# A down projection on one Trainium2 core: weights as the moving operand, and the last twelve feature tiles as six pairs with seven products each

## The chip, the cores and the metric

The kernel runs on one core of one Trainium2 chip. Its five engines have a queue each: TensorE (PE in the profile, its weight loads PEld), VectorE (DVE), ScalarE (ACT), GpSimd (POOL) and SyncE (SP, which issues most transfers). The metric is the device time of the whole program in microseconds (us); lower is better. Runs of one kernel lie within about 0.2% of each other.

## The reference

One layer of a hybrid trunk for 512 tokens of 1024 features, all in float32: token mixers, cross-attention, then a SwiGLU feed-forward block and a final RMSNorm. The change lies in the last two:

```python
gate, up = _split_cols(rmsnorm(x, norm_ffn[l]) @ w_gate_up[l], (D_FF, D_FF))   # D_FF = 2816
x = x + (jax.nn.silu(gate) * up) @ w_down[l]
return rmsnorm(x, norm_final)
```

With 128 rows to a tile, the 2816 features between the two projections are 22 tiles (`KF`), the 1024 output features are 8 (`KD`), the 512 tokens are 4 (`NT`).

## The kernel before, in words

**Precision.** Each float32 product is made of three fp32r matmuls on split operands: `hi` is the operand rounded by a ScalarE copy (L111), `lo` is what is left, a VectorE subtraction (L113), and the product is hi·hi + hi·lo + lo·hi. `split` does both. So every weight tile that arrives by DMA (`raw`) costs ScalarE one pass and VectorE one pass before TensorE can use it (`whi`, `wlo`, three buffers of 128x1024 each, as `raw`).

**Order.** TensorE's order is the order in which the program is written. `drive` runs a generator of matmul steps and, at every step, advances the pending generators once; a `side` generator is advanced at a given rate. ScalarE's, VectorE's and SyncE's instructions are placed by a scheduler at build time, and each engine then works strictly in that order.

**Gate and up projections.** Four feature tiles are computed plainly; tiles 4 to 21 are eighteen *units* (`unit`, L1211 on), each of seven Strassen products of 4 x 3 matmuls with 256 moving columns (L1221 to L1223), whose weights come in quarters. VectorE forms the sums of products from PSUM and at the end writes `gu` (L1252), one feature tile on the partitions by 512 tokens. `gu_split` splits these into `guh`, `gul`.

**Down projection, features on partitions.** For each of the eight output tiles j, `block_steps` (L128 on) runs 22 x 3 matmuls (L137 to L139): the stationary operand is a 128x128 weight tile, the moving one the 512 tokens of `guh` or `gul`. Weights come in three pieces of 8, 8 and 6 tiles. After a block, `wd_after` adds the residual (L1289) and squares the sum for the norm, and scales it by the gain (L1291). The last block is done in two halves of 256 tokens (`wd_last`), so that the end of the first half is hidden by the second.

**Final norm.** The features are on the partitions, so the sum of squares over features is itself made by matmuls with ones (L1307), then VectorE (L1311), GpSimd's power (L1313), a matmul that spreads the row over the partitions (L1317), four VectorE multiplications (L1321) and four output transfers (L1322), for each half.

**Buffers.** `G("a")`, `G("b")`, `G("c")` are pools of 16, 16 and 8 tiles of 128x512, `V` one of 20; `TMP` takes small rotating pools, of which "c" has three tiles. PSUM has eight banks: `PM` 3, `PS` 2, `PD` 3.

Of the kernel before, what the change touches and what calls it, by code (L numbers as in the profile page):

```python
# [40 lines left out]
def hybrid_block(  # L41
    ctx: ExitStack,
    tc: tile.TileContext,
    xT, xN, memT, memN, consts, wz0, wz, wq, wk, wv, wqb, wkb, wvb, wga, wgb,
    w_a, w_b, bias, w_o, w_mq, w_mk, w_mv, w_mo, w_g, w_u, w_d, outT,
):
    nc = tc.nc
    ctx.enter_context(tc.manual_schedule(engines={mybir.EngineType.PE}))
# [26 lines left out]
    def TMP(name, tag, bufs=None, shape=(P, T), dt=F32, pool=None):  # L75
        return (pool or tp).tile(list(shape), dt, tag="t" + tag, bufs=bufs or TB[tag], name=nm(name))
# [12 lines left out]
    def PS(name):  # L89
        return PSUM("ms", name)  # L90
# [16 lines left out]
    def gain(c, k):  # L107
        return cst[:, c + k : c + k + 1]
# [19 lines left out]
    def block_steps(ps, src, act, kt=KD, pieces=None, n=slice(0, T), eng=None):  # L128

        pieces = pieces or [(0, kt)]  # L130
        w = n.stop - n.start
        for a, b in pieces:
            hi, lo = weights(src[:, a:b, :] if (a, b) != (0, kt) else src, b - a, P, eng)
            for k in range(a, b):
                xh, xl = act[k]
                first, last = k == 0, k == kt - 1
                nc.tensor.matmul(out=ps[:, :w], lhsT=hi[:, k - a, :], rhs=xh[:, n], start=first, stop=False)  # L137
                nc.tensor.matmul(out=ps[:, :w], lhsT=hi[:, k - a, :], rhs=xl[:, n], start=False, stop=False)  # L138
                nc.tensor.matmul(out=ps[:, :w], lhsT=lo[:, k - a, :], rhs=xh[:, n], start=False, stop=last)  # L139
                yield  # L140
# [1142 lines left out]
    x4 = x3
    acc4 = TMP("acc", "acc")
    PIECES = [(0, 8), (8, 16), (16, KF)]
    dps = {}

    def wd_after(j):
        nc.vector.tensor_tensor(out=x4[j], in0=dps[j], in1=x4[j], op=ALU.add)  # L1289
        square_sum(acc4, x4[j], j)  # L1290
        nc.scalar.activation(x4[j], x4[j], AF.Copy, scale=gain(C_FIN, j))  # L1291
        yield

    def wd_last(j, tok, ps, sq):
        yield from block_steps(ps, w_d[j], gu, kt=KF, pieces=PIECES, n=tok)
        nc.vector.tensor_tensor(out=x4[j][:, tok], in0=ps[:, :H], in1=x4[j][:, tok], op=ALU.add)
        q = TMP("sq", "th")
        nc.scalar.activation(q[:, :H], x4[j][:, tok], AF.Square)
        sq.append(q)
        nc.scalar.activation(x4[j][:, tok], x4[j][:, tok], AF.Copy, scale=gain(C_FIN, j))  # L1300

    def final(tok, sq):
        yield from wait(6)
        ps = [PS("r4") for _ in range(2)]
        for i, q in enumerate([acc4[:, tok]] + sq):
            for tt in range(2):
                nc.tensor.matmul(out=ps[tt][:, 0:1], lhsT=q[:, tt * P : tt * P + P], rhs=ones[:, 0:1],  # L1307
                                 start=(i == 0), stop=(i == len(sq)))
        var, rs = SM("r4", 2), SM("r4", 2)
        for tt in range(2):  # L1310
            nc.vector.tensor_scalar(out=var[:, tt : tt + 1], in0=ps[tt][:, 0:1], scalar1=1.0 / D, scalar2=EPS,  # L1311
                                    op0=ALU.mult, op1=ALU.add)
        nc.gpsimd.tensor_tensor(out=rs, in0=var, in1=mhalf[:, :2], op=ALU.pow)  # L1313
        yield from wait(4)
        pr = PS("row4")
        for tt in range(2):
            nc.tensor.matmul(out=pr[:, tt * P : tt * P + P], lhsT=rs[:, tt : tt + 1].to_broadcast([P, P]), rhs=ident,  # L1317
                             start=True, stop=True)
        for i in (3, 0, 1, 2):
            x = x2t[i][:, :, tok]  # L1320
            nc.vector.tensor_tensor(out=x, in0=x, in1=pr[:, :H].unsqueeze(1).to_broadcast([P, 2, H]), op=ALU.mult)  # L1321
            (nc.scalar if i in (0, 2) else nc.sync).dma_start(out=outT[i][:, :, tok], in_=x)  # L1322

    wd = series(w_d, dps, gu, wd_after, range(KD - 1), kt=KF, pieces=PIECES)
    side = gu_splits(range(13, KF))
    drive(wd[0], side=side)
    drive(*wd[1:])
    for hf in range(2):
        tok, sq = slice(hf * H, hf * H + H), []
        drive(*[(wd_last(j, tok, PM("wd"), sq), None) for j in (KD - 1,)])  # L1330
        pending.append(final(tok, sq))
# [73 lines left out]
```

## Time and profile before

| | us |
|---|---|
| median of three runs | 1207.29 (1205.94 to 1208.83) |
| the profiled execution | 1206.24 |
| its span, from the first to the last instruction | 1204.5 |
| eighteen units, each | 10.1 |
| first matmul of the down projection | at 1071.56 |
| seven whole blocks | 1071.5 to 1176.7 |
| the last block, in two halves | 1176.7 to 1194.0 |
| end of the last matmul of the projection to the end of the span | 10.5 |

Times inside the execution count from the first instruction. The profile names an instruction by source line, engine, operation and tiles (out<-in). A busy TensorE is not a TensorE at its peak: matmuls overlap, so that the duration of one (390 ns) is longer than the distance between two starts, and it is the distance that adds up.

### The profile page before, as it was taken

To read this page: it belongs to the slowest core of one execution; us is meant where nothing else is said; L and a number is where in the kernel's file an instruction comes from. 1 tells how busy PE (TensorE), PEld (TensorE's weight loads), DVE (VectorE), ACT (ScalarE), POOL (GpSimd) and SP (SyncE) were. 2 spreads that over 40 slices of the span, in tenths; PEclk is the share of its full clock that TensorE was granted. 3 is DMA by queue.
4 is the path that set the end of the run, shared out by engine and by line. 5 is a ranking of instruction groups with operands and counts; after the bars stand their busy time and mean duration, and the time that the engine had idled before them with its cause. 6 is when DMAs were issued, how large, how long until landed. Compare 5 with 4: busy or idle time off the path is not lost.

```text
span 1204.5 us, 19433 instructions
## 1 busy us (share of the span) xinstructions
PE 1190.0 (99%) x7461; PEld 1040.0 (86%) x7461; DVE 757.4 (63%) x1550; ACT 579.8 (48%) x1195; POOL 140.4 (12%) x140
## 2 busy tenths in 40 slices
PE   9999999999999999999999999999999999999997
PEld 8788888899998887777788898888889999998886
DVE  5977783356543487875465564446888998892223
ACT  7573334355742376765333453335544555462222
POOL 0031331120110000000022200002021111100000
PEclk9999999999999999999999999999999999999998
DMA  8253335111343432223324453113267777633333
GB/s 284 88 167 119 127 109 138 62 54 58 125 142 125 164 114 81 88 89 113 112 98 125 130 175 122 54 36 123 79 169 195 188 179 189 160 107 103 97 96 101
DMA packets 72044, 147.04 MB, mean 122 GB/s; under 512 B 18928, under 2 KB 27536, under 8 KB 71952
## 3 DMA queue, kind: packets, MB, share of 16 engines
q1 hardware_dynamic: 65680, 135.32, 35.9%
q0 software_dynamic: 5184, 9.44, 4.6%
q8 instruction: 58, 0.95, 0.3%
q10 hardware_dynamic: 1088, 1.05, 0.3%
q14 instruction: 34, 0.28, 0.1%
HBM read 137.90 MB, written 7.88 MB: 121 GB/s over the span
## 4 chain that ended last, share of the span: by engine, by line
PE 92%; DVE 3%; DMA 2%; ACT 1%; issue 1%; POOL 0%; POOLq 0%; SPq 0%; DVEq 0%; ACTq 0%
PE g L137 6%; PE g L139 6%; PE g L138 6%; PE fp L1223 5%; PE fp L1222 5%; PE fp L1221 5%; PE nat L162 3%; PE nat L164 2%; PE nat L163 2%; PE pt L821 2%; PE ob L829 2%; PE qa L137 1%; DMA raw<-in_wz 1%; PE kb L137 1%; PE ff L137 1%; PE gb L137 1%
## 5 line engine op out<-in xcount | busy, mean ns | idle before, releaser
L111 ACT ACTIVATE whi<-raw 128x1024 fp32r<-128x1024 f32 (+4 forms) x220 | 203.1, 931 | 309.6 <-PE g L138 91.3
L113 DVE TENSOR_TENSOR wlo<-raw,whi 128x1024 fp32r<-128x1024 f32 (+4 forms) x206 | 225.1, 1098 | 152.2 <-ACT whi L111 151.6
L1223 PE MATMUL fp<-fh,wlo 128*128 128x256 f32 x504 | 142.7, 283 | 0.1
L1221 PE MATMUL fp<-fh,whi 128*128 128x256 f32 x504 | 142.6, 283 | 0.0
L1222 PE MATMUL fp<-fl,whi 128*128 128x256 f32 x504 | 142.6, 283 | 0.0
L1223 PEld LDWEIGHTS fp<-fh,wlo 128*128 128x128 f32 x504 | 96.7, 192 | 0.3 <-DVE wlo L113 0.3
L1221 PEld LDWEIGHTS fp<-fh,whi 128*128 128x128 f32 x504 | 96.8, 192 | 0.0
L1222 PEld LDWEIGHTS fp<-fl,whi 128*128 128x128 f32 x504 | 96.8, 192 | 0.0
L111 ACT ACTIVATE whi<-fs 128x512 fp32r<-128x512 f32 x72 | 42.4, 624 | 54.0 <-PE fp L1222 28.4
L203 POOL TENSOR_TENSOR acc<-acc,sq 128x512 f32<-128x512 f32 x18 | 28.8, 1600 | 299.0 <-ACT sq L202 167.8
L138 PE MATMUL g<-gul,whi 128*128 128x512 f32 x154 | 60.1, 390 | 0.0
L139 PE MATMUL g<-guh,wlo 128*128 128x512 f32 x154 | 60.1, 390 | 0.0
L137 PE MATMUL g<-guh,whi 128*128 128x512 f32 x154 | 60.1, 390 | 0.0
L162 PE MATMUL nat<-whi,hh 128*128 128x256 f32 x192 | 57.1, 298 | 0.4 <-DVE conv L391 0.4
L164 PE MATMUL nat<-wlo,hh 128*128 128x256 f32 x192 | 54.3, 283 | 0.0
L163 PE MATMUL nat<-whi,hl 128*128 128x256 f32 x192 | 54.2, 282 | 0.0
L113 DVE TENSOR_TENSOR wlo<-fs,whi 128x512 fp32r<-128x512 f32 x72 | 48.0, 686 | 5.5 <-ACT whi L111 4.7
L799 ACT ACTIVATE P<-P,mx 128x128 f32<-128x128 f32 (+1 forms) x64 | 35.9, 561 | 30.0 <-DVE mx L797 29.8
L113 POOL TENSOR_TENSOR wlo<-raw,whi 128x1024 fp32r<-128x1024 f32 x14 | 34.0, 2428 | 105.3 <-ACT whi L111 105.3
L162 PEld LDWEIGHTS nat<-whi,hh 128*128 128x128 f32 x192 | 36.7, 191 | 0.9 <-issue 0.6
L163 PEld LDWEIGHTS nat<-whi,hl 128*128 128x128 f32 x192 | 36.7, 191 | 0.0
L164 PEld LDWEIGHTS nat<-wlo,hh 128*128 128x128 f32 x192 | 36.6, 191 | 0.0
(419 smaller groups left out, 3275.4 us busy)
## 6 DMA issues: line engine op xcount, KB each, us to landing
raw<-in_w_g SPq DMA_DIRECT2D x22, 512.0 KB, 4.4
fs<-in_w_u SPq DMA_DIRECT2D x36, 256.0 KB, 2.9
raw<-in_w_d SPq DMA_DIRECT2D x18, 512.0 KB, 3.5
raw<-in_w_u SPq DMA_DIRECT2D x18, 256.0 KB, 5.0
fs<-in_w_u POOLq DMA_DIRECT2D x18, 256.0 KB, 5.8
fs<-in_w_g POOLq DMA_DIRECT2D x18, 256.0 KB, 5.6
raw<-in_wk SPq DMA_DIRECT2D x8, 512.0 KB, 4.0
raw<-in_wga SPq DMA_DIRECT2D x8, 512.0 KB, 3.7
```

The lines of the kernel that those rows point to most:

```text
L111: nc.scalar.activation(hi, src, AF.Copy, scale=1.0 if scale is None else scale)
L113: (eng or nc.vector).tensor_tensor(out=lo, in0=src, in1=hi.bitcast(F32), op=ALU.subtract)
L137: nc.tensor.matmul(out=ps[:, :w], lhsT=hi[:, k - a, :], rhs=xh[:, n], start=first, stop=False)
L138: nc.tensor.matmul(out=ps[:, :w], lhsT=hi[:, k - a, :], rhs=xl[:, n], start=False, stop=False)
L139: nc.tensor.matmul(out=ps[:, :w], lhsT=lo[:, k - a, :], rhs=xh[:, n], start=False, stop=last)
L162: nc.tensor.matmul(out=o, lhsT=xh[:, tok], rhs=hi[:, kw, :], start=(k == 0), stop=False)
L163: nc.tensor.matmul(out=o, lhsT=xl[:, tok], rhs=hi[:, kw, :], start=False, stop=False)
L164: nc.tensor.matmul(out=o, lhsT=xh[:, tok], rhs=lo[:, kw, :], start=False, stop=(k == KD - 1))
L799: nc.scalar.activation(pr, pr, AF.Exp, scale=-1.0, bias=mx, accum_out=rs[:, t : t + 1])
L1221: nc.tensor.matmul(out=o, lhsT=hi[:, k, :], rhs=xh, start=k == 0, stop=False)
L1222: nc.tensor.matmul(out=o, lhsT=hi[:, k, :], rhs=xl, start=False, stop=False)
L1223: nc.tensor.matmul(out=o, lhsT=lo[:, k, :], rhs=xh, start=False, stop=k == 3)
```

## The change

The stationary operand is now the activation, 128 features by 128 tokens, and the moving operand 512 output features of the weights (`w_d` is laid out as 22 tiles of 128x1024). The output has tokens on the partitions: eight banks hold four token tiles times two feature halves, called quads a, b, c, d of two banks each, and all stay open through the whole projection.

- `plain_down`: feature tiles 0 to 9, each times eight banks, three matmuls each (`triple`).
- Tiles 10 to 21 are six pairs. A pair is a 2x2 block product: 256 tokens by 128 features by 512 outputs a piece, done with seven products (of two token tiles, three matmuls each) where eight stood. `down_first` has four products for each pair, `down_second` the other three; `middle` moves sums between quads from PSUM with VectorE.
- Activation sums are prepared by `preps` beside `plain_down`; weight sums (`t3`, the second half of `raw`, `t2s`) by VectorE inside `down_first`.
- `take_part` empties the eight banks of the plain sum into `part` tiles together with the residual, so that the residual must have tokens on partitions too: `natural_x3` transposes it by 32 TensorE transposes, four in each of eight units, and ScalarE copies them back.
- The final norm works per partition: ScalarE squares and sums along the row (`accum_out`), VectorE adds, GpSimd takes the power, and one scale per row half follows. It runs for each token tile by itself (`final`); the output is stored as 512x1024.

Where instructions went. VectorE in a plain block of the down projection, before; `x` is the residual tile, `g` the PSUM bank of the block:

```order
L1289 TENSOR_TENSOR x_0_6700<-g_11587,x_0_6700 128x512
L113 TENSOR_TENSOR wlo_11775<-raw_11772,whi_11774 128x768
L113 TENSOR_TENSOR wlo_11800<-raw_11797,whi_11799 128x1024
L113 TENSOR_TENSOR wlo_11835<-raw_11832,whi_11834 128x1024
L1289 TENSOR_TENSOR x_0_6700<-g_11708,x_0_6700 128x512
```

and in `down_first` of the change, from the third pair's first sum on; `w_2427` and `w_2436` are the lower right weight tiles (`w22`) of the third and fourth pair, `w_2416`, `w_2425` and `w_2434` the lower left ones (`w21`) of the first, second and third, `t_` is `t3`:

```order
L1389 TENSOR_TENSOR t_2428_12186<-raw_12184,w_2427_12185 128x512
L1409 TENSOR_TENSOR t2s_12089<-t2s_12089,w_2416_12123 128x512
L1409 TENSOR_TENSOR t2s_12145<-t2s_12145,w_2425_12169 128x512
L1390 TENSOR_TENSOR raw_12184<-raw_12184 128x512
L1394 TENSOR_TENSOR t2s_12191<-raw_12184,w_2427_12185 128x512
L113 TENSOR_TENSOR wlo_12193<-raw_12184,whi_12192 128x1024
L1389 TENSOR_TENSOR t_2437_12232<-raw_12230,w_2436_12231 128x512
L113 TENSOR_TENSOR wlo_12198<-t_2428_12186,whi_12197 128x512
L113 TENSOR_TENSOR wlo_12198<-t2s_12191,whi_12197 128x512
L1390 TENSOR_TENSOR raw_12230<-raw_12230 128x512
L1409 TENSOR_TENSOR t2s_12191<-t2s_12191,w_2434_12215 128x512
```

Where a block of 66 matmuls had four VectorE rows, a pair of 24 matmuls has seven: one of 1024 columns and six of 512. `w_2436` lies in the buffer that `w_2425` held, so its transfer can start only after the third row.

TensorE in a unit, in the second product of the unit, before:

```order
L1221 MATMUL fp_9575<-fh_8605,whi_9516 128x256
L1222 MATMUL fp_9575<-fl_8606,whi_9516 128x256
L1223 MATMUL fp_9575<-fh_8605,wlo_9517 128x256
L1221 MATMUL fp_9575<-fh_8607,whi_9516 128x256
L1222 MATMUL fp_9575<-fl_8608,whi_9516 128x256
L1223 MATMUL fp_9575<-fh_8607,wlo_9517 128x256
```

and in the change; `x3n` is the PSUM bank that takes the transposed residual tile `x_1`:

```order
L1221 MATMUL fp_9587<-fh_8605,whi_9528 128x256
L1222 MATMUL fp_9587<-fl_8606,whi_9528 128x256
L1223 MATMUL fp_9587<-fh_8605,wlo_9529 128x256
L1301 MATMUL x3n_9599<-ident,x_1_6701 128x128 x4
L1221 MATMUL fp_9587<-fh_8607,whi_9528 128x256
L1222 MATMUL fp_9587<-fl_8608,whi_9528 128x256
L1223 MATMUL fp_9587<-fh_8607,wlo_9529 128x256
```

Four transposes stand between two matmul triples of one product; eight units have them.

The diff, cut to its core:

```diff
-            tag = "c" if j < 5 or j == KF - 1 else "a" if j < 13 else "b"
+            tag = "c" if j < 5 else "a"
...
+    NPL, NSP = 10, 6
+    HOME = ("bbbbbbb", "bbbbbbb", "vvvvvvv", "vvvvvvv", "aaaaaab", "vvvvccb")
+    def preps(js):
+        for i in js:
+            top, bot = gf[NPL + 2 * i], gf[NPL + 2 * i + 1]
+            x11, x21, x12, x22 = top[:, lh], top[:, rh], bot[:, lh], bot[:, rh]
...
+            tt(out=u[:, lh], in0=x21, in1=x22, op=ALU.subtract)
+            tt(out=u[:, rh], in0=u[:, lh], in1=x11, op=ALU.subtract)
+            split(tiles[0], tiles[1], u)
+            tt(out=v[:, lh], in0=x11, in1=x21, op=ALU.subtract)
+            tt(out=v[:, rh], in0=u[:, rh], in1=x12, op=ALU.add)
+            split(tiles[6][:, lh], tiles[6][:, rh], x11)
+            split(tiles[2], tiles[3], v)
+            split(tiles[4], tiles[5], bot)
...
+    def natural_x3(j):
+        pt = PS("x3n")
+        for t in range(NT):
+            nc.tensor.transpose(out=pt[:, t * P : t * P + P], in_=x3[j][:, t * P : t * P + P], identity=ident)
+        yield
+        nc.scalar.activation(x3[j], pt, AF.Copy)
...
+        if 5 <= j < 5 + KD:
+            pending.append(seq(wait(6), natural_x3(j - 5)))
...
+    def triple(o, act, w, t, **kw):
+        for i, (x, y) in enumerate(((0, 0), (1, 0), (0, 1))):
+            nc.tensor.matmul(out=o, lhsT=act[x][:, tok], rhs=w[y], start=start and i == 0, stop=stop and i == 2, **kw)
...
+    def plain_down():
+        for k in range(NPL):
+            raw, hi, lo = (pair_tile(t) for t in ("raw", "whi", "wlo"))
+            nc.sync.dma_start(out=raw, in_=w_d[k].rearrange("p (x f) -> p x f", x=2))
+            split(hi, lo, raw)
+            for n, q in enumerate("ccbbaadd" if k else "acdacdbb"):
...
+                triple(banks[q][t], gu[k], (hi[:, hf, :], lo[:, hf, :]), tok0 + t, start=k == 0, stop=k == NPL - 1)
+                if k == NPL - 1 and n % 2:
+                    pending.append(take_part(q))
...
+    def down_first():
+        for i in range(NSP):
+            ra, w22, t3 = pair_tile("raw"), TMP("w22", "c"), TMP("t3", "th")
...
+            tt(out=t3, in0=a[1], in1=w22, op=ALU.add)
+            tt(out=a[1], in0=a[0], in1=a[1], op=ALU.add)
+            split(ha, la, ra)
+            tt(out=t2s[i], in0=a[1], in1=w22, op=ALU.add)
+            split(hb[:, 1, :], lb[:, 1, :], t3)
+            split(hb[:, 0, :], lb[:, 0, :], t2s[i])
+            for q, act, hi, lo, x in (("c", op["x11"], ha, la, 0), ("b", op["s1"], ha, la, 1),
+                                      ("a", op["s3"], hb, lb, 1), ("d", op["s2"], hb, lb, 0)):
+                for t in range(2):
+                    triple(banks[q][t], act, (hi[:, x, :], lo[:, x, :]), t, start=i == 0, stop=i == NSP - 1)
...
+                if q == "b":
+                    nc.sync.dma_start(out=w21, in_=bot[:, :T])
+                    tt(out=t2s[i], in0=t2s[i], in1=w21, op=ALU.add)
...
+    def middle():
+        for t in range(2):
+            tt(out=keep[2 + t], in0=p["b"][t], in1=keep[2 + t], op=ALU.subtract)
+        for t in range(2):
+            tt(out=keep[t], in0=p["d"][t], in1=keep[t], op=ALU.add)
+        for t in range(2):
+            for n, o, op in (("a", t, ALU.add), ("d", t, ALU.subtract), ("d", 2 + t, ALU.add), ("b", t, ALU.subtract)):
+                tt(out=r[n][t], in0=r[n][t], in1=keep[o], op=op)
...
+    def last_sum(n, x):
+        if q != "d":
+            tt(out=r, in0=r, in1=banks[q][n % 2], op=ALU.add)
+        nc.scalar.activation(junk, r, AF.Square, scale=1.0 / 32, accum_out=ssq[n][:, x : x + 1])
+        tt(out=r, in0=r, in1=grow[x], op=ALU.mult)
...
+    def final(n):
+        nc.vector.scalar_tensor_tensor(out=v, in0=ssq[n][:, 0:1], scalar=EPS, in1=ssq[n][:, 1:2],
+                                       op0=ALU.add, op1=ALU.add)
+        nc.gpsimd.tensor_tensor(out=rs, in0=v, in1=mhalf[:, :1], op=ALU.pow)
+        nc.scalar.activation(r[1], r[1], AF.Copy, scale=rs)
+        nc.scalar.dma_start(out=outN[n * P : n * P + P, T:], in_=r[1])
+        nc.vector.tensor_scalar(out=r[0], in0=r[0], scalar1=rs, scalar2=None, op0=ALU.mult)
+        nc.sync.dma_start(out=outN[n * P : n * P + P, :T], in_=r[0])
...
+    drive((plain_down(), None), side=seq(gu_splits(range(6, NPL)), preps(range(NSP))), rate=0.55, delay=2)
+    drive((down_first(), middle()))
+    drive((down_second(), final(1)))
```

`down_second` takes, in this order: the fourth weight product (`t2s`) of pairs 0 and 1 into quad a; the lower weights of pair 0 into quads b and c; the fourth of pair 2; the lower weights of pair 1; and so on, with the last three pairs' lower weights token tile by token tile at the end. Removed are `wd_after`, `wd_last` and the old `final` with everything said of them above.

More of the change, by code (lines that the diff above doesn't have):

```diff
@@ L1277, in hybrid_block @@
             pending.append(seq(wait(8), gu_splits([j - 9])))
+        if 5 <= j < 5 + KD:
+            pending.append(seq(wait(6), natural_x3(j - 5)))
         if j == KF - 2:
-            pending.append(seq(wait(10), gu_splits(range(5, 9)), wait(8), gu_splits(range(9, 13))))
+            pending.append(seq(wait(10), gu_splits([5])))
     flush()
[L1283 to L1291, printed above, removed]
-        yield
@@ L1294, in wd_last @@
[L1294 to L1331, printed above, removed]
+    banks = {"a": [PM("wda"), PM("wda")], "c": [PD("wdc"), PD("wdc")], "d": [PS("wdd"), PS("wdd")],
+             "b": [PM("wdb"), PD("wdb")]}
+    quad = {"c": (0, 0), "b": (0, 1), "a": (2, 0), "d": (2, 1)}
@@ new lines, in hybrid_block, with halves, pair_tile @@
+    part = {n: [G("c", "part") for _ in range(2)] for n in "cb"}
+    keep = [TMP("keep", "ti") for _ in range(4)]
+    grow = [TMP("grow", t) for t in ("rrow", "acc")]
+    def halves(t):
+        return [t[:, x, :] for x in range(2)]
+    def pair_tile(tag):
+        return wp.tile([P, 2, T], F32 if tag == "raw" else F32R, tag=tag, bufs=3, name=nm(tag))
+    def triple(o, act, w, t, **kw):
+        tok = slice(t * P, t * P + P)
+        start, stop = kw.pop("start"), kw.pop("stop")
+        for i, (x, y) in enumerate(((0, 0), (1, 0), (0, 1))):
+            nc.tensor.matmul(out=o, lhsT=act[x][:, tok], rhs=w[y], start=start and i == 0, stop=stop and i == 2, **kw)
@@ new lines, in old, with view, take_part @@
+    def old(q, t, x):
+        tok0, hf = quad[q]
+        o = (tok0 + t) * P
+        return x2t[2 * hf + x][:, :, o : o + P]
+    def view(t, x):
+        return t[:, x * H : x * H + H].rearrange("p (e f) -> p e f", e=2)
+    def take_part(q):
+        if q in "ad":
+            part[q] = [G("a", "part") for _ in range(2)]
+        for t in range(2):
+            r, ps = part[q][t], banks[q][t]
+            if q in "cb":
+                for x in range(2):
+                    tt(out=view(r, x), in0=view(ps, x), in1=old(q, t, x), op=ALU.add)
+            else:
+                nc.scalar.activation(r, ps, AF.Copy)
+        yield
+        if q in "ad":
+            for t in range(2):
+                for x in range(2):
+                    tt(out=view(part[q][t], x), in0=view(part[q][t], x), in1=old(q, t, x), op=ALU.add)
+                yield
@@ new lines, in hybrid_block @@
+    t2s = {}
+    def down_first():
+        for x in range(2):
+            nc.sync.dma_start(out=grow[x], in_=gfin[:, x * T : x * T + T])
+        for i in range(NSP):
+            top, bot = w_d[NPL + 2 * i], w_d[NPL + 2 * i + 1]
+            ra, w22, t3 = pair_tile("raw"), TMP("w22", "c"), TMP("t3", "th")
+            nc.sync.dma_start(out=ra, in_=top.rearrange("p (x f) -> p x f", x=2))
+            nc.sync.dma_start(out=w22, in_=bot[:, T:])
+            a = halves(ra)
+            tt(out=t3, in0=a[1], in1=w22, op=ALU.add)
+            tt(out=a[1], in0=a[0], in1=a[1], op=ALU.add)
+            t2s[i] = G("a", "t2s")
+            ha, la = pair_tile("whi"), pair_tile("wlo")
+            split(ha, la, ra)
+            tt(out=t2s[i], in0=a[1], in1=w22, op=ALU.add)
+            hb, lb = pair_tile("whi"), pair_tile("wlo")
+            split(hb[:, 1, :], lb[:, 1, :], t3)
+            split(hb[:, 0, :], lb[:, 0, :], t2s[i])
+            op = ops_[i]
+            for q, act, hi, lo, x in (("c", op["x11"], ha, la, 0), ("b", op["s1"], ha, la, 1),
+                                      ("a", op["s3"], hb, lb, 1), ("d", op["s2"], hb, lb, 0)):
+                for t in range(2):
+                    triple(banks[q][t], act, (hi[:, x, :], lo[:, x, :]), t, start=i == 0, stop=i == NSP - 1)
+                    if i == NSP - 1 and q in "ca":
+                        nc.scalar.activation(keep[t + 2 * (q == "a")], banks[q][t], AF.Copy)
+                    yield
+                if q == "b":
+                    w21 = TMP("w21", "c")
+                    nc.sync.dma_start(out=w21, in_=bot[:, :T])
+                    tt(out=t2s[i], in0=t2s[i], in1=w21, op=ALU.add)
@@ new lines, in middle @@
+    def middle():
+        p, r = banks, part
+        for t in range(2):
+            tt(out=keep[2 + t], in0=p["b"][t], in1=keep[2 + t], op=ALU.subtract)
+        yield from wait(12)
+        for t in range(2):
+            tt(out=keep[t], in0=p["d"][t], in1=keep[t], op=ALU.add)
+            yield
+        for t in range(2):
+            for n, o, op in (("a", t, ALU.add), ("d", t, ALU.subtract), ("d", 2 + t, ALU.add), ("b", t, ALU.subtract)):
+                tt(out=r[n][t], in0=r[n][t], in1=keep[o], op=op)
+                yield
@@ new lines, in down_second, with fourth, load, one @@
+    def down_second():
+        ws, w4 = {}, []
+        def fourth(i):
+            if i % 2 == 0:
+                w4[:] = pair_tile("whi"), pair_tile("wlo")
+            w = tuple(z[:, i % 2, :] for z in w4)
+            split(w[0], w[1], t2s[i])
+            for t in range(2):
+                triple(banks["a"][t], ops_[i]["x22"], w, t, start=False, stop=i == NSP - 1, skip_group_check=True)
+                yield
+        def load(i):
+            raw, hi, lo = (pair_tile(t) for t in ("raw", "whi", "wlo"))
+            nc.sync.dma_start(out=raw, in_=w_d[NPL + 2 * i + 1].rearrange("p (x f) -> p x f", x=2))
+            split(hi, lo, raw)
+            ws[i] = hi, lo
+        def one(i, t, x):
+            hi, lo = ws[i]
+            q, o = (("c", "x12"), ("b", "s4"))[x]
+            triple(banks[q][t], ops_[i][o], (hi[:, x, :], lo[:, x, :]), t, start=False, stop=i == NSP - 1,
+                   skip_group_check=True)
+            yield
+        def both(i, t):
+            yield from one(i, t, 1)
+            yield from one(i, t, 0)
+        yield from fourth(0)
+        yield from fourth(1)
+        for i in range(NSP - 3):
+            load(i)
+            for t in range(2):
+                yield from both(i, t)
+            if i + 2 < NSP:
+                yield from fourth(i + 2)
+        for i in range(NSP - 1, NSP):
+            yield from fourth(i)
+        pending.append(seq(final(2), final(3)))
+        for i in range(NSP - 3, NSP):
+            load(i)
+            yield from both(i, 0)
+        pending.append(final(0))
+        for x in (1, 0):
+            for i in range(NSP - 3, NSP):
+                yield from one(i, 1, x)
@@ new lines, in hybrid_block @@
+    ssq = {}
+    def last_sum(n, x):
+        lh_ = n < 2
+        q = ("c", "b")[x] if lh_ else ("a", "d")[x]
+        r = part[q][n % 2]
+        if q != "d":
+            tt(out=r, in0=r, in1=banks[q][n % 2], op=ALU.add)
+        if n not in ssq:
+            ssq[n] = SM("ssq", 2, tag="ssq", bufs=4)
+        junk = TMP("sqj", "th")
+        nc.scalar.activation(junk, r, AF.Square, scale=1.0 / 32, accum_out=ssq[n][:, x : x + 1])
+        tt(out=r, in0=r, in1=grow[x], op=ALU.mult)
+        return r
@@ new lines, in final @@
+    def final(n):
+        r = {}
+        for x in (1, 0):
+            r[x] = last_sum(n, x)
+        yield
+        v, rs = SM("r4", 1, tag="r4v", bufs=4), SM("r4", 1, tag="r4s", bufs=4)
+        nc.vector.scalar_tensor_tensor(out=v, in0=ssq[n][:, 0:1], scalar=EPS, in1=ssq[n][:, 1:2],
[5 more added lines that the diff above has]
+        nc.sync.dma_start(out=outN[n * P : n * P + P, :T], in_=r[0])
+        yield
@@ L1403 @@
     got = r.results[0]["out_0"]
[L1404 removed]
+    return _np.ascontiguousarray(got).reshape(1, T, D)
```

26 lines of the change are left out of this document (21 added, 5 removed).

## The prediction

> **What bounds the kernel now.** First the page: each engine's share of the span, and the span in 40 slices of 30.1 us.
>
> ```profile
> PE 1190.0 (99%) x7461; PEld 1040.0 (86%) x7461; DVE 757.4 (63%) x1550; ACT 579.8 (48%) x1195; POOL 140.4 (12%) x140
> ...
> PE   9999999999999999999999999999999999999997
> DVE  5977783356543487875465564446888998892223
> PEclk9999999999999999999999999999999999999998
> ```
>
> TensorE is full until the last slice, at full clock; VectorE is at 8 to 9 tenths in the units and at 2 to 3 in the down projection. Then the waits of TensorE over the last 440 us, longest first:
>
> ```profile
> PE row L1317 <- POOL r L1313: 1.0, 1, 1.0
> PE r L1307 <- ACT sq L1298: 0.7, 1, 0.7
> ```
>
> Only the final norm keeps it waiting, so before that the time is the number of matmuls times their distance. For the distance, the busy time by windows: whole blocks, the last block, the tail (columns: us, then busy us and instructions of PE, PEld, DVE, ACT, POOL, then clock, DMA share, GB/s).
>
> ```profile
> 1071.50:1176.70 105.20, 105.20 (x464) 86.80 (x464) 37.09 (x44) 33.76 (x43) 6.48 (x5) 1.00 0.33 98
> 1176.70:1194.00 17.30, 17.30 (x147) 17.26 (x147) 8.21 (x12) 5.99 (x8) 2.00 (x2) 1.00 0.25 82
> 1194.00:1204.50 10.50, 2.07 (x13) 1.60 (x11) 3.22 (x7) 0.92 (x2) 0.70 (x1) 0.64 0.41 142
> ```
>
> Seven blocks are 462 matmuls of 512 columns in 105.2 us: one every 0.2277 us. The last block, 132 of 256 columns and some of the norm's, takes 17.3. The projection takes 122.5 us, the tail 10.5.
>
> **Part by part: TensorE.** Afterwards 10 tiles x 8 banks x 3 = 240 matmuls and 6 pairs x 7 products x 2 x 3 = 252, all of 512 columns with a new stationary tile each, as now. 492 x 0.2277 = 112.0 us, 10.5 less: 36 matmuls fewer are 8.2, and 66 long ones for the last block (15.0 for 17.3) are 2.3.
>
> **The 32 transposes** are new in the full units. The same form stands in the attention part (start, us, what):
>
> ```profile
> 504.25 0.60 PE L821 MATMUL pt<-ident,P 128*128 128x128 f32 x4
> 504.61 0.37 PE L794 MATMUL sc<-kA,qA 128*128 128x256 f32 x1
> ...
> 508.06 0.38 PE L821 MATMUL pt<-ident,P 128*128 128x128 f32 x2
> 508.19 0.48 PE L794 MATMUL sc<-kA,qA 128*128 128x512 f32 x1
> ```
>
> Four hold TensorE for 0.36 us, two for 0.13, so 32 cost between 2.1 and 2.9; I take 2.9, from the group of the same size. One lasts longer than that:
>
> ```profile
> L821 PE MATMUL pt<-ident,P x160: 270/272/330, 441.0 to 577.9; 128*128 128x128 f32 x160
> ```
>
> but they overlap. The Trainium skill ("TensorE: Matmul & The Clock Gate", Part 4: PE-mode transpose) gives about 275 ns for a transpose in one kernel's context; taken as the price of each it would be 8.8 us, 5.9 more. By that rule the trace agrees on the duration and not on the price of a group. ScalarE's copy of each result (0.62 us) waits in order for the transposes, and the weight splits behind it wait too. What hides that is ScalarE's idle time in a unit, in brackets:
>
> ```profile
> 968.01 1.15 ACT L111 ACTIVATE whi<-fs 128x512 fp32r<-128x512 f32 x2 [1.42 <-issue]
> 970.89 1.15 ACT L111 ACTIVATE whi<-fs 128x512 fp32r<-128x512 f32 x2 [1.73 <-issue]
> ```
>
> 1.4 to 1.7 us twice and more in 10: nothing. With that cover gone, 0.6 us x 8 units would be 5.
>
> **VectorE in the pairs.** Here the cover is thin. The prices, by kind (busy us, mean ns):
>
> ```profile
> L113 DVE TENSOR_TENSOR wlo<-raw,whi 128x1024 fp32r<-128x1024 f32 x18 | 22.0, 1224 | 58.8 <-ACT whi L111 58.8
> L113 DVE TENSOR_TENSOR wlo<-fs,whi 128x512 fp32r<-128x512 f32 x32 | 21.4, 686 | 2.4 <-ACT whi L111 1.9 <-PE fp L1222 0.4
> L111 ACT ACTIVATE whi<-raw 128x1024 fp32r<-128x1024 f32 x18 | 19.1, 1061 | 52.3 <-PE g L138 45.2 <-issue 3.3 <-PE wd L138 2.4
> L111 ACT ACTIVATE whi<-fs 128x512 fp32r<-128x512 f32 x32 | 18.8, 624 | 24.3 <-PE fp L1222 14.4 <-issue 9.9
> L1289 DVE TENSOR_TENSOR x<-g,x 128x512 f32<-128x512 f32 x7 | 4.8, 691 | 13.9 <-PE g L139 13.9
> ```
>
> and how close they follow each other where VectorE is full:
>
> ```profile
> 1004.78 0.68 DVE L1191 TENSOR_TENSOR fs<-fs,raw 128x512 f32<-128x512 f32 x1
> 1005.50 0.69 DVE L1192 TENSOR_TENSOR fs<-raw,fs 128x512 f32<-128x512 f32 x1
> 1006.11 1.28 DVE L113 TENSOR_TENSOR wlo<-raw,whi 128x512 fp32r<-128x512 f32 x2
> ...
> 1010.40 0.41 DVE L1247 TENSOR_TENSOR fU<-fU,fp 128x256 f32<-128x256 f32 x1
> 1010.73 0.41 DVE L1248 TENSOR_TENSOR fcc<-fW,fp 128x256 f32<-128x256 f32 x1
> ```
>
> L1192 reads what L1191 wrote and starts 0.72 us after it; the next row, which needs neither, starts 0.61 later; 256 columns take 0.33. So I count 0.60 for 512 columns, 0.33 for 256, 0.72 where a row reads the one ahead, and 1.13 for 1024 (1.22 less the same 0.09). The Trainium skill ("VectorE: DVE Perf Modes", The DRAIN you can't avoid) has it that the next operation doesn't start until the pipeline is empty; by that rule every row costs its whole duration, and the time is that of the first rival below. The trace agrees for the dependent row only.
>
> A pair: 1.13 + 6 x 0.60 + 0.12 = 4.85 us of VectorE in 24 x 0.2277 = 5.46 of TensorE. It keeps up, with 0.6 a pair. Three places are tight.
>
> (1) Entering: VectorE can't run ahead, for the first pair's second split goes into the buffer of plain tile 8 (from 0), released 24 matmuls or 5.46 us before the plain part ends; with 0.2 for the matmul's own end and ScalarE's pass of 0.62, VectorE starts 4.6 ahead of that end. Up to the first pair's last `lo` stand 14 rows of 256 (the plain sums with the residual), 5 of 512 and one of 1024: 4.62 + 3.0 + 1.13 = 8.75 us, to 4.15 after the end. TensorE wants it after 20 matmuls, 4.55. It fits by 0.4.
>
> (2) `w22` of pairs four to six waits for a buffer that `t2s += w21` frees, three rows ahead of the sum `t3` that needs it (0.60, 0.72 for the one that reads it, 1.13, and about 0.5 of waiting for ScalarE's pass of 1.06 between, an estimate): 2.9 us. The transfers:
>
> ```profile
> raw<-in_w_d SPq DMA_DIRECT2D x18, 512.0 KB, 3.5
> ...
> fs<-in_w_u SPq DMA_DIRECT2D x36, 256.0 KB, 2.9
> raw<-in_w_u SPq DMA_DIRECT2D x18, 256.0 KB, 5.0
> ```
>
> 256 KB land in 2.9 where the queue is quiet, in 5.0 in the busy units. The pairs are quiet: just in time.
>
> (3) In `down_second` the first lower weights go into a buffer that is free when pair six is half done, 2.7 us before its end; 0.2 and ScalarE's pass of 1.06 later, 1.45 before the end, VectorE goes on. Then stand 1.13 + 4 x 0.62 (PSUM, `middle`) + 8 x 0.60 + 1.13 = 9.5 us ahead of the second lower weights' `lo`, that is 8.1 after the pair's end, where TensorE wants it after 32 matmuls, 7.3. It waits 0.8.
>
> I take 1.0 us of waiting in all: bounds are 0 and the 3.8 that full durations give. `preps` and the splits beside it (6 rows of 1024, 18 of 512, 28 of 256: 26.8 us of VectorE in the 54.6 of 240 matmuls) hide.
>
> **The tail.** Now it is this chain:
>
> ```profile
> 1194.08 0.42 DVE L1296 TENSOR_TENSOR x<-wd,x 128x256 f32<-128x256 f32 x1 [1.41 <-PE wd L139]
> 1194.60 0.42 ACT L1298 ACTIVATE sq<-x 128x256 f32<-128x256 f32 x1 [8.16 <-DVE x L1296]
> 1195.95 0.70 POOL L1313 TENSOR_TENSOR r<-r,mhalf 128x2 f32<-128x2 f32 x1 [6.86 <-DVE r L1311]
> 1197.88 2.48 DVE L1321 TENSOR_TENSOR x<-x,row 128x512 f32<-128x512 f32 x4 [2.01 <-PE row L1317]
> ```
>
> From the end of L1321 (1200.36) to the span's end are 4.1 us of output. The two small matmul steps and three of four multiplications go. Afterwards: about 1.0 for VectorE's queue (it serves token tiles 2, 3 and 0 in the last 10 us), the sum 0.69, ScalarE's square 0.62, the add (under 0.2), the power 0.70, the scale 0.62 and 4.1 for the output are 7.9, and 6 handovers of some 0.15 make 8.9; I take 9.0, 1.5 less.
>
> **Sum.** -10.5 + 1.0 + 2.9 - 1.5 = -8.1 on the profiled execution's 1206.24 (span 1204.5): 1198.1. The median of the runs lies 1.05 above that execution: 1199.2.
>
> **The rivals.**
> - *VectorE pays whole durations.* A pair is then 1.22 + 6 x 0.69 = 5.36 of 5.46; entering takes 14 x 0.41 + 5 x 0.69 + 1.22 = 10.4 and is late by 1.3; place (3) takes 10.7 and waits 2.0; with no slack left the late transfers of place (2) show, 0.5. That is 3.8, 2.8 over the forecast, and the tail's queue adds 0.7: 1202.7. For it: many rows of a pair read the one ahead. Against: rows that don't start 0.60 to 0.61 apart.
> - *Slower: the `w22` transfers lead.* VectorE then stands 3 x (landing - 2.9 - 0.6), TensorE behind it. At 5.0 us that is 4.5, 1203; it decides the sign from 6.2 on; at 7.5 it is 12: 1210. For it: SyncE issues in order, and three half loads stand between whole ones. Against: 3.5 us for 512 KB in this very stage.
> - *Transposes cost their duration*: 32 x 0.272 = 8.7, 5.8 more: 1205.0, no change. Against it: the 0.36 us.
> - *Everything fits*: no waiting, tail without queue (8.0), transposes 2.1: 2.8 less, 1196.4.
>
> **Chances.** Forecast 0.50, whole durations 0.20, everything fits 0.14, transposes 0.05, `w22` 0.06, and 0.05 for some cost in the units that eats the gain. Measurements of this kernel tell about 0.2% (2.4 us) from no change. Faster are the first three, 0.84; slower `w22`, 0.06; the rest 0.10. The range takes the first three, with the runs' own spread of 1.4 about the outer ones: 1195.0 to 1204.2.
>
> **What would show it.** The plain part at 54.6 us; TensorE waiting for VectorE's `wlo` near the second lower weights and little elsewhere; units longer by 0.36 in eight of eighteen; the last output issued some 5.5 us after the last matmul. Wrong if TensorE waits over 4 us in the pairs, for `wlo` behind `t3` (then `w22`) or behind back-to-back rows (then durations), or if the units grow by over 0.5 each.

## The result, and the profile after

The change runs in 1198.06 us (median of four runs, 1197.57 to 1198.93), the kernel before in 1206.80 (four runs, 1205.94 to 1208.83): a ratio of 0.9926, with a 95% interval of 0.9909 to 0.9943. The forecast was 1199.2. The profiled execution took 1197.57 us and has a span of 1195.9.

The page: engines' shares, and the span in 40 slices of 29.9 us, to be held against the same rows of before.

```profile
PE 1180.9 (99%) x7367; PEld 1029.3 (86%) x7367; DVE 805.2 (67%) x1652; ACT 598.0 (50%) x1238; POOL 135.1 (11%) x136
...
PE   9999999999999999999999999999999999999997
DVE  5977783356543388875365564546788898899687
PEclk9999999999999999999999999999999999999999
```

TensorE is as full as before. VectorE's last four slices, 2 to 3 tenths before, are now 6 to 9. Then the busy time by windows, cut at the first matmul of the units, at the first one of the projection, at the pairs, at `down_second` and at the end of the last matmul:

```profile
888.89:1074.10 185.21, 185.11 (x1546) 184.90 (x1544) 164.03 (x312) 99.73 (x196) 28.11 (x32) 1.00 0.70 177
1074.10:1128.97 54.87, 54.87 (x242) 45.06 (x241) 40.46 (x77) 23.89 (x38) 0.00 (x0) 1.00 0.30 97
1128.97:1162.06 33.09, 33.09 (x145) 27.04 (x144) 29.85 (x47) 15.95 (x26) 0.00 (x0) 1.00 0.54 167
1162.06:1187.75 25.69, 25.27 (x109) 20.00 (x107) 23.04 (x38) 13.55 (x25) 1.51 (x2) 1.00 0.30 103
1187.75:1195.90 8.15, 0.00 (x0) 0.00 (x0) 2.78 (x6) 2.06 (x4) 1.47 (x2) 0.67 0.34 129
```

and of before the row that answers to the first:

```profile
889.78:1071.56 181.78, 181.68 (x1513) 181.47 (x1512) 163.24 (x312) 97.18 (x192) 27.95 (x32) 1.00 0.70 176
```

The stages side by side, in us:

| | forecast | before | after | difference |
|---|---|---|---|---|
| units, with the transposes | +2.9 | 181.78 | 185.21 | +3.43 |
| projection, first start to last end | -9.5 | 122.48 | 113.65 | -8.83 |
| tail | -1.5 | 10.46 | 8.15 | -2.31 |
| sum | -8.1 | 314.72 | 307.01 | -7.71 |

The two executions also differ by 0.89 us ahead of the units (888.89 against 889.78), where no instruction of the change stands. A start that is compared between executions carries that: the projection's first matmul is only 2.54 us later, and the units are 3.43 longer. So the stages are compared by their lengths, not by when they begin.

TensorE's waits in units, projection and tail, and those of its weight loads in the projection:

```profile
PE wdb L1338 <- DVE wlo L113: 0.4, 1, 0.4
PEld wdb L1338 <- DVE wlo L113: 0.8, 1, 0.8
```

One wait, at the place (3) of the prediction: the matmuls stand idle 0.4 us there, the weight loads 0.8.

### The profile page after: what moved, and what is told of

It reads as the page before. It is cut to its first block, busy times and chain, and to the rows that moved or that the text cites. A ratio compares the mean times of both kernels' runs of the same rounds, so it can differ in the third digit from the quotient of the medians.

```text
span 1195.9 us, 19401 instructions
## 1 busy us (share of the span) xinstructions
PE 1180.9 (99%) x7367; PEld 1029.3 (86%) x7367; DVE 805.2 (67%) x1652; ACT 598.0 (50%) x1238; POOL 135.1 (11%) x136
## 4 chain that ended last, share of the span: by engine, by line
PE 90%; issue 4%; DVE 3%; DMA 2%; ACT 1%; SPq 0%; POOL 0%; POOLq 0%; DVEq 0%
PE fp L1223 5%; PE fp L1221 5%; PE fp L1222 5%; PE g L137 3%; PE g L139 3%; PE g L138 3%; PE nat L162 3%; PE wdb L1338 3%; PE nat L163 2%; PE nat L164 2%; PE wda L1338 2%; PE wdc L1338 2%; PE wdd L1338 2%; PE pt L821 2%; PE ob L829 2%
## 5 line engine op out<-in xcount | busy, mean ns | idle before, releaser
L111 ACT ACTIVATE whi<-raw 128x1024 fp32r<-128x1024 f32 (+3 forms) x215 | 199.7, 937 | 272.3 <-issue 65.2
L113 DVE TENSOR_TENSOR wlo<-raw,whi 128x1024 fp32r<-128x1024 f32 (+3 forms) x201 | 221.6, 1107 | 99.6 <-ACT whi L111 98.7
L799 ACT ACTIVATE P<-P,mx 128x128 f32<-128x128 f32 (+1 forms) x64 | 35.9, 561 | 30.1 <-DVE mx L797 29.9
L203 POOL TENSOR_TENSOR acc<-acc,sq 128x512 f32<-128x512 f32 x12 | 21.6, 1800 | 172.7 <-issue 131.0
L797 DVE CUSTOM_DVE_ANT_0 P<-sc,bias 128x128 f32<-128x128 f32 (+1 forms) x64 | 31.0, 484 | 4.8 <-PE sc L795 4.2
L1189 POOL DMA_DIRECT2D fs<-in_w_g x18 | 15.8, 875 | 120.8 <-DVE fs L1191 33.6
L137 PE MATMUL qa<-hh,whi 128*128 128x512 f32 x64 | 28.7, 448 | 0.0
```

Of the source, the lines that this page charges most:

```text
L111: nc.scalar.activation(hi, src, AF.Copy, scale=1.0 if scale is None else scale)
L113: (eng or nc.vector).tensor_tensor(out=lo, in0=src, in1=hi.bitcast(F32), op=ALU.subtract)
L799: nc.scalar.activation(pr, pr, AF.Exp, scale=-1.0, bias=mx, accum_out=rs[:, t : t + 1])
```

## The experiments

### Without the transposes

```diff
-        if 5 <= j < 5 + KD:
-            pending.append(seq(wait(6), natural_x3(j - 5)))
```

> The change without the 32 transposes of the residual and without ScalarE's eight copies of them, so that the residual that is added has features where tokens belong. The theory, by the 0.32 us that a group of four added between the units' matmuls: the first matmul of the projection comes 2.5 us earlier than with the change (about 1071.6 instead of 1074.1), the time is about 1195.5. The rival, by the 272 ns that one transpose lasts: 8.7 us earlier, about 1189.4.

Measured: 1195.01 us, ratio to the kernel before 0.9898 (0.9879 to 0.9916), 3 to 4 us under the change. Its units:

```profile
888.25:1070.05 181.80, 181.70 (x1513) 181.49 (x1512) 163.35 (x312) 95.48 (x188) 27.93 (x32) 1.00 0.71 179
```

181.80 is the length before to 0.02, so the transposes, with ScalarE's copies, cost 185.21 - 181.80 = 3.41 us, 0.427 a group and 0.107 each. The projection's first matmul comes 4.05 us earlier, but 0.64 of that lies ahead of the units. The rival's 8.7 falls; but the theory's 2.5, and the bounds of 2.1 to 2.9 in the prediction, were too low. Why shows in the change's rows round a group (start, us, what):

```profile
932.82 0.28 PE L1223 MATMUL fp<-fh,wlo 128*128 128x256 f32 x1
932.94 0.60 PE L1301 MATMUL x3n<-ident,x 128*128 128x128 f32 x4
933.29 0.37 PE L1221 MATMUL fp<-fh,whi 128*128 128x256 f32 x1
933.50 0.28 PE L1222 MATMUL fp<-fl,whi 128*128 128x256 f32 x1
933.62 0.28 PE L1223 MATMUL fp<-fh,wlo 128*128 128x256 f32 x1
```

From the first transpose to the next matmul's start are 0.35 us, which is what the prediction read in the attention part (0.36). But that matmul holds TensorE for 0.21 where its neighbours hold it for 0.12: part of the group's cost comes out behind it. The attention part of the kernel before shows the same in the row behind the two that the prediction read:

```profile
504.81 0.28 PE L795 MATMUL sc<-klz,qA 128*128 128x256 f32 x1
```

The matmul at 504.61 holds TensorE for 0.20, also at 256 columns. With the 0.08 over 0.12 the group costs 0.44, and eight of them 3.5, close to the 3.41. The distance must be taken to the second start behind a group.

### All plain, tokens on the partitions

`plain_all` takes the place of `plain_down`, `down_first`, `middle` and `down_second`; its first 19 feature tiles run like this, the last three token tile by token tile.

```diff
-    drive((down_first(), middle()))
-    drive((down_second(), final(1)))
+        for k in range(KF - 3):
+            for n, q in enumerate("ccbbaadd" if k else "acdacdbb"):
+                triple(banks[q][t], gu[k], (hi[:, hf, :], lo[:, hf, :]), tok0 + t, start=k == 0, stop=False)
...
+    drive((plain_all(), final(1)), side=gu_splits(range(6, KF)), rate=0.55, delay=2)
```

> All 22 feature tiles plain, with tokens on the partitions, the weights moving, the transposes and the new norm as in the change; no pairs, no sums of weights or activations, no sums between banks. The theory (36 more matmuls at 0.228 us, and no wait or longer distance in the pairs to set against them): the projection takes 528 x 0.2277 = 120.2 us where the change takes 113.65, the tail as with the change or 0.3 longer: about 1204.8, 2 us under the kernel before. The rival that the seven products are eaten by what VectorE and ScalarE do for them: within 1.5 us of the change, about 1198 to 1199.5.

Measured: 1207.50 us, ratio 0.9998 (0.9984 to 1.0013): no different from the kernel before, and 9 us over the change. In its profiled execution the stages ahead of the units, which are the same, took 5.9 us longer than in the change's (its granted clock was 0.83 from 80 to 100 us, 1.00 in the change's), so it is read from the units on: units, projection, tail.

```profile
894.74:1079.94 185.20, 185.09 (x1545) 184.89 (x1544) 164.05 (x312) 101.37 (x200) 27.93 (x32) 1.00 0.69 175
1079.94:1200.26 120.32, 120.32 (x530) 99.00 (x528) 41.66 (x58) 30.76 (x42) 1.50 (x2) 1.00 0.26 86
1200.26:1209.60 9.34, 0.00 (x1) 0.00 (x0) 4.43 (x12) 3.55 (x8) 1.64 (x2) 0.65 0.37 140
```

The projection is as expected: 528 matmuls, 120.32 us. The tail is 1.2 longer than the change's (its last sums are two VectorE rows of 256 columns each instead of one of 512, and one of them waits for a tile that an output still reads). The total missed the expected 1204.8 by 2.7 us: the longer tail is 0.9 to 1.2 of that, the rest lies in the ten runs' spread (1204.59 to 1211.37), which is wider than the change's. From the units on it takes 314.86 us, the kernel before 314.72. So the turned operands alone bring nothing: 2.2 us off the projection (the last block in 512 columns) and 1.1 off the tail are paid back by 3.4 for the transposes. The gain is that of the seven products: 113.65 for 120.32, -6.67 of the 8.2 that 36 matmuls are worth. The rival that they are eaten falls.

### Two more VectorE rows in each pair

```diff
             tt(out=t2s[i], in0=a[1], in1=w22, op=ALU.add)
+            for _ in range(2):
+                tt(out=xtra, in0=t2s[i], in1=grow[0], op=ALU.add)
```

> The change with two more VectorE sums of 128x512 in each pair of the first products; nobody reads their result. It asks how much of a pair VectorE has left. The theory (rows start 0.60 us apart): a pair is 4.85 + 1.20 = 6.05 us of VectorE in 5.46 to 5.58 of TensorE, so TensorE waits 0.5 to 0.6 a pair, less what slack there is at the start, 2.0 to 4.0 us in all: about 1200 to 1202. The rival (rows cost their whole duration): 5.36 + 1.38 = 6.74, 1.2 us a pair, 7 us or more: about 1205 or later. Waits of TensorE would name VectorE's lo of the pair weights in both.

Measured: 1201.29 us, ratio 0.9953 (0.9939 to 0.9967), 3.2 over the change; the projection takes 117.37 us, 3.72 more. TensorE's waits and those of its weight loads:

```profile
PE wdc L1339 <- DVE wlo L113: 1.6, 4, 0.7
PE wdb L1339 <- DVE wlo L113: 1.0, 1, 1.0
```

```profile
PEld wdc L1339 <- DVE wlo L113: 3.3, 4, 1.1
PEld wdb L1339 <- DVE wlo L113: 1.4, 1, 1.4
PEld wdd L1339 <- DVE wlo L113: 0.5, 1, 0.5
```

and one pair of VectorE, from one second extra row (L1397) to the next:

```profile
1143.71 0.69 DVE L1397 TENSOR_TENSOR xtra<-t2s,grow 128x512 f32<-128x512 f32 x1
1144.32 0.69 DVE L113 TENSOR_TENSOR wlo<-t,whi 128x512 fp32r<-128x512 f32 x1
1144.92 0.69 DVE L113 TENSOR_TENSOR wlo<-t2s,whi 128x512 fp32r<-128x512 f32 x1
1145.52 0.69 DVE L1390 TENSOR_TENSOR t<-raw,w 128x512 f32<-128x512 f32 x1
...
1147.92 0.70 DVE L1395 TENSOR_TENSOR t2s<-raw,w 128x512 f32<-128x512 f32 x1
1148.68 1.23 DVE L113 TENSOR_TENSOR wlo<-raw,whi 128x1024 fp32r<-128x1024 f32 x1
1149.83 0.69 DVE L1397 TENSOR_TENSOR xtra<-t2s,grow 128x512 f32<-128x512 f32 x1
```

Rows that last 0.69 start 0.60 apart, and this pair takes 6.12 us where the prediction's prices make 6.05. That is the theory's case (2.0 to 4.0 us more), not that of whole durations (7 or more). It also shows how thin the cover is: two rows of 0.6 us a pair are enough to make VectorE the bound.

### Where the longer distances in the pairs come from

The projection came out 0.65 us over the forecast's 113.0 though it waited less. The first rows of pairs 1 to 5 in the change (counted from 0, as in `HOME`; the prediction's third pair is pair 2 here):

```profile
1134.41 0.61 PE L1338 MATMUL wdc<-whi,op 128*128 128x512 f32 x2
...
1139.86 0.62 PE L1338 MATMUL wdc<-whi,op 128*128 128x512 f32 x2
...
1145.45 0.63 PE L1338 MATMUL wdc<-whi,op 128*128 128x512 f32 x2
...
1151.06 0.62 PE L1338 MATMUL wdc<-whi,op 128*128 128x512 f32 x2
...
1156.50 0.62 PE L1338 MATMUL wdc<-whi,op 128*128 128x512 f32 x2
```

Pairs 1 and 4 take 5.45 and 5.44 us, pairs 2 and 3 take 5.59 and 5.61: 0.227 and 0.233 us a matmul, at the same granted clock of 1.00 and with no wait between. Pairs 2 and 3 keep their activation tiles in the pool `V` (`HOME`), and so do the plain tiles 0 to 2, which are as slow (0.233; tiles 3 to 9 are at 0.227). By the addresses of the build, all other activation and weight tiles start 864 bytes past a multiple of 2048, those of `V` 1664. Six runs move tiles in memory with unused bytes and change nothing else.

```diff
+    pad = sp.tile([P, 8], F32, tag="pad", bufs=1, name="pad")
+    nc.gpsimd.memset(pad, 0.0)
```

> The change with 32 bytes of padding ahead of one pool of 20 activation tiles, so that these tiles start at the same place modulo 64 bytes as all other operands; nothing else differs. In the change's trace matmuls with an operand in this pool start 0.2333 us apart (plain tiles 0 to 2, pairs 2, 3 and most of 5), the others 0.2268. If it is where the tile starts that does it: 0.2268 everywhere, 180 x 0.0065 = 1.2 us off the projection (113.65 to 112.5), and up to 576 x 0.0062 = 3.6 off three earlier projections that take operands from the pool: 1193.3 to 1196.9. If it is the pool's place high in the memory, or what else runs at these times (VectorE's rows, transfers): no change, 1198.1.

Measured: 1197.21 us, ratio 0.9917 (0.9896 to 0.9937). The projection didn't move (113.76 us), so the first theory falls for stationary operands; stages with a moving operand from the pool came down, by less than expected (to 0.230 a matmul). Neither theory as stated. The next two use 224 bytes (56 columns for 8), the second 32 more ahead of the other pools:

> The change with 224 bytes of padding ahead of the same pool in place of the 32 of the run before it: its tiles then start at the same place modulo 1024 bytes as the other activation and weight tiles (all of those stand 864 bytes past a multiple of 2048, the pool's now 1888). The run with 32 bytes left stationary operands from the pool at 0.233 us and brought moving ones from 0.2333 to about 0.2299. If the distance depends on how the tiles stand to each other modulo 1024 or less: 0.227 for both kinds, the projection 1.2 us shorter (113.26 to about 112.1 from first to last start), the three earlier projections 3.5 us shorter, about 1193.4. If the start modulo 64 is all: as the run with 32 bytes, about 2 us under the change, 1196, and nothing in the projection. If the pool's place in the memory counts: no change beyond that of the run with 32.

> As the run with 224 bytes, and in addition 32 bytes ahead of all the other pools, so that every activation and weight tile starts at a multiple of 128 bytes (896 past a multiple of 2048) and all stand to each other as in that run. If only how the tiles stand to each other counts: the same time as that run. If the start modulo 64 or 128 itself counts, all 512-column matmuls move from 0.2268 us, up or down: 0.006 either way would be some 20 us over the kernel's 3500 such matmuls.

Measured: 1193.07 us, ratio 0.9889 (0.9873 to 0.9905), and 1192.62, 0.9894 (0.9872 to 0.9916). Four stages of the change: attention's output projection, cross-attention, the plain gate and up tiles, the down projection.

```profile
590.95:636.20 45.25, 45.25 (x197) 36.44 (x196) 26.50 (x22) 13.68 (x18) 9.04 (x7) 1.00 0.29 96
636.20:791.80 155.60, 155.60 (x910) 136.79 (x909) 82.81 (x125) 66.78 (x108) 14.94 (x9) 1.00 0.37 118
842.30:888.89 46.59, 46.59 (x209) 37.78 (x208) 37.94 (x76) 22.82 (x45) 4.73 (x5) 1.00 0.38 107
1074.10:1187.75 113.65, 113.23 (x494) 92.10 (x492) 93.34 (x160) 53.39 (x87) 1.51 (x2) 1.00 0.37 119
```

and the same with 224 bytes:

```profile
590.88:634.88 44.00, 44.00 (x198) 36.50 (x197) 26.43 (x22) 13.69 (x18) 9.00 (x7) 1.00 0.29 94
634.88:789.41 154.53, 154.53 (x909) 136.82 (x908) 82.74 (x125) 66.68 (x108) 14.94 (x9) 1.00 0.38 120
839.78:885.18 45.40, 45.40 (x209) 37.83 (x208) 37.93 (x76) 22.93 (x45) 4.73 (x5) 1.00 0.39 108
1070.38:1182.96 112.58, 112.02 (x494) 92.11 (x492) 93.35 (x160) 53.32 (x87) 1.50 (x2) 1.00 0.37 119
```

-1.25, -1.07, -1.19 and -1.07 us: 3.5 in the first three, as expected, and 1.07 in the projection for the expected 1.2. There every plain tile and pair now runs at 0.227 to 0.228 us a matmul; the wait at place (3) is 0.14 longer. This version is faster than both kernels. Moving everything by 32 bytes more changes nothing that can be measured. Three more settle what counts: 96 bytes (24 columns) ahead of the pool, the kernel before so padded (152 columns), and 224 bytes ahead of all the other pools instead of the one.

> The change with 96 bytes of padding: the pool's tiles then start at the same place as the others modulo 128 bytes, but not modulo 256. If 128 is the measure: the time of the run with 224 bytes, 1193, first to last start of the projection 112.2 us. If 256, 512 or 1024 is: little or nothing in the projection (113.3), about 1196 to 1198.

> The kernel before, with padding (608 bytes) ahead of the same pool, so that its tiles start at the same place modulo 1024 bytes as all the others. In it 72 matmuls of the down projection's seven whole blocks and last block have a moving operand from the pool, and so have the three earlier projections. The theory: 3.5 us there and about 0.4 in the down projection, about 1203.3; the change so padded (1193.1) is then still some 10 us, 0.8%, under it, so the change's gain does not hang on where the pool lies. The rival that only stationary operands or only the changed kernel care: no change, 1207.

> The change with 224 bytes of padding ahead of all the other pools instead of the one: the pool of 20 tiles then starts at the very address that it had in the run with 224 bytes ahead of it, but the others have moved along, so that the tiles stand to each other as in the change. If it is how the two operands of a matmul stand to each other: the change's distances again, 0.2333 with an operand from the pool, first to last start of the projection 113.3 us, about 1198. If it is the pool's own address: 112.2 and about 1193 to 1194.

Measured: 1197.20 us with 96 bytes (0.9920, 0.9905 to 0.9935), its projection 113.2 from first to last start, so standing alike modulo 128 bytes isn't enough. The kernel before takes 1202.09 us with its pool moved (0.9957, 0.9941 to 0.9974), 4.8 less for the expected 4. The change so padded is 9.0 under it, 8.2 by the two ratios: the change's gain doesn't hang on the pool. With all the others moved as well, 1198.09 us (0.9934, 0.9918 to 0.9951) and 113.29 from first to last start: the pool lay at the very address of the fast run, and was slow again. So it is how a matmul's tiles stand to each other in memory that counts, modulo something of more than 128 and at most 1024 bytes; which of 256, 512 and 1024 wasn't tried. That the two tiles of one matmul are what counts, and not the pool against some third tile, is read from which matmuls are slow; no run separates the two.

### Another order in the norm

```diff
-        tt(out=r, in0=r, in1=grow[x], op=ALU.mult)
         return r
...
         nc.gpsimd.tensor_tensor(out=rs, in0=v, in1=mhalf[:, :1], op=ALU.pow)
+        for x in (1, 0):
+            if n != 1 or x:
+                tt(out=r[x], in0=r[x], in1=grow[x], op=ALU.mult)
...
+            nc.vector.scalar_tensor_tensor(out=r[0], in0=r[0], scalar=rs, in1=grow[0], op0=ALU.mult, op1=ALU.mult)
```

> The change with another order in the final norm: the sum of the two halves' squares and GpSimd's power are issued ahead of the multiplication by the gain, and for the last token tile one VectorE operation does the gain and the scale together. Nothing before the last few microseconds differs. The theory that the tail is one chain through VectorE's queue (the add, the square, the power, the scale): the last scale ends about 0.9 us earlier (0.6 to 1.1), the tail is 7.3 us instead of 8.15. The rival that the end is set by the eight output transfers of 256 KB on their queues: no change, 8.15.

Measured: 1198.79 us, ratio 0.9939 (0.9922 to 0.9957): no different from the change. The change's last chain (its last matmul ends at 1187.75):

```profile
1188.20 0.68 DVE L1478 TENSOR_TENSOR part<-part,wdc 128x512 f32<-128x512 f32 x1
1188.72 0.72 ACT L1495 ACTIVATE part<-part,r 128x512 f32<-128x512 f32 x1 [1.55 <-POOL r L1494]
...
1189.35 0.61 ACT L1482 ACTIVATE sqj<-part 128x512 f32<-128x512 f32 x1
...
1190.09 0.69 DVE L1483 TENSOR_TENSOR part<-part,grow 128x512 f32<-128x512 f32 x1 [0.81 <-ACT sqj L1482]
1190.69 0.15 DVE L1492 SCALAR_TENSOR_TENSOR r<-ssq 128x1 f32<-128x1 f32 x1
1190.93 0.54 POOL L1494 TENSOR_TENSOR r<-r,mhalf 128x1 f32<-128x1 f32 x1 [2.24 <-DVE r L1492]
1191.51 0.72 ACT L1495 ACTIVATE part<-part,r 128x512 f32<-128x512 f32 x1 [1.45 <-POOL r L1494]
```

and that of the new order (its last matmul ends at 1188.21, its span is 1196.1):

```profile
1188.58 0.72 ACT L1497 ACTIVATE part<-part,r 128x512 f32<-128x512 f32 x1 [0.95 <-POOL r L1493]
1188.66 0.68 DVE L1478 TENSOR_TENSOR part<-part,wdc 128x512 f32<-128x512 f32 x1
...
1190.71 0.54 POOL L1493 TENSOR_TENSOR r<-r,mhalf 128x1 f32<-128x1 f32 x1 [2.16 <-DVE r L1491]
1191.28 0.72 ACT L1497 ACTIVATE part<-part,r 128x512 f32<-128x512 f32 x1 [0.85 <-POOL r L1493]
1191.29 0.75 DVE L1500 SCALAR_TENSOR_TENSOR part<-part,r,grow 128x512 f32<-128x512 f32 x1 [0.66 <-POOL r L1493]
```

From the last matmul's end to the end of the last scale are 4.48 us in the change and 3.83 here, 0.65 less; but from there to the span's end 3.67 and 4.06, so 0.26 is left of it. The expected 0.9 fell, and so did the rival's nothing. The earlier scale is there, but VectorE still starts the last add 0.45 after the last matmul, behind other rows. Why the output takes 0.4 longer stays open: its last two transfers are issued 0.02 us apart, those of the change 0.24, but no run tests whether that is the reason.

## Why the prediction was right, point by point

- **TensorE, -10.5.** Right. 240 plain matmuls took 54.87 us (forecast 54.6), and all 528 in the plain run 120.32 (528 x 0.2277 is 120.2), which also bears out the 2.3 for the last block. What the forecast did not see: its 0.2277 is a mean over matmuls at 0.2268 and some at 0.2333. In the change 180 of 492 take their stationary tile from `V` (72 for plain tiles 0 to 2, 84 for pairs 2 and 3, 24 for pair 5), 1.1 us by the run with 224 bytes; before, 72 matmuls had a moving tile from `V`.
- **Transposes, +2.9.** The mechanism was right, they overlap; the size was off: 3.41. The step that failed is the reading of 0.36 for a group, up to the next start alone; the next row of the same trace had the rest. The Trainium skill ("TensorE: Matmul & The Clock Gate", Part 4: PE-mode transpose) gives about 275 ns for one; by that rule the trace agrees on the duration (272 in both kernels), and the run without the transposes shows 107 ns as the price.
- **VectorE in the pairs, +1.0.** Right within a few tenths: TensorE waited once, 0.8 us by its weight load and 0.7 by the starts of its matmuls, at place (3), for the 0.8 forecast there. Entering the pairs (place 1) cost nothing, as worked out. At place (2) VectorE waited 1.1 us once for `w22`, and TensorE not at all: the slower rival had the right place, at a small part of its price. The reading behind this place was wrong. The two rows of 2.9 and 5.0 us for 256 KB both stand in the units of the kernel before, so they don't set a quiet queue against a busy one, and in the pairs such transfers landed in 2.9 to 4.1 us. That "just in time" cost nothing is in part luck. Beside the plain tiles VectorE was busy for 40.5 us, not the 26.8 that the prediction counted, and it hid all the same. The rival of whole durations fell by the two added rows: the Trainium skill's rule that the next operation waits for an empty pipeline ("VectorE: DVE Perf Modes", The DRAIN you can't avoid) doesn't hold for rows of 0.69 that start 0.60 apart. The same section adds that an operation that is not held starts earlier, which the prediction left out; with that the trace agrees.
- **Tail, -1.5.** It was -2.3, 8.15 for 9.0, with errors on both sides. VectorE's queue holds the last add up by 0.45 us, not 1.0, the output took 3.67, not 4.1, and the handovers at the end of the chain are 0.03 to 0.09, not 0.15. Against that, the sum left two pieces out: the last half's square starts 0.47 after its add ends, behind another tile's scale on ScalarE, and the multiplication by the gain (L1483) holds the add of the two halves' squares up by 0.60. The last output was issued 4.5 us after the last matmul, for some 5.5 forecast.
- The errors partly cancel: transposes +0.5, projection +0.7, tail -0.8, and 0.9 of the profiled difference lies ahead of the units. The stages' sum, -7.7 for -8.1, is closer than its terms, and that is luck.

## What to carry to other kernels

Price a group of foreign instructions on TensorE to the second start behind it, and compare executions by the lengths of stages that hold the same instructions. Where a matmul's distance changes with no wait and no clock to blame, look at which pool its operands lie in and at the addresses. And before calling an algebraic saving good, run the new layout without it: here the layout alone gained nothing, and the seven products all of it.

## What the runs showed of the hardware that was not expected

- **Tiles that stand differently in memory slow the matmul.** 512-column fp32r matmuls started 0.2268 us apart where both operands stood alike modulo 1024 bytes. Where one did not they started 0.2333 apart, or 0.230 to 0.233 with the paddings of 32 and 96 bytes. The padding that makes them alike is worth 5.0 us of the change and 4.8 of the kernel before. It is the relation, not an address. The Trainium skill ("SBUF — State Buffer", Who interferes with whom) lists two independent read ports for TensorE, one for the moving operand and one for weight loads; by the distances here, where the one tile lies still matters to the other. What the two meet in, no run shows.
- **Four transposes among matmuls of another shape cost 0.427 us**, 0.35 to the next start and the rest in the matmul behind them.
